# Start addresses of matmul operands in SBUF, brought to one offset modulo 2 KB

## The chip, the cores and the metric

One Trainium2 chip, one of its cores. The metric is the device time of one execution of the whole program in microseconds, as the median of repeated runs: 3694.65 us before (3 runs, 3694.28 to 3696.64). The profile comes from one more execution.

## What is computed

Two blocks follow each other on 256 tokens of width 2048, in float32. Cut to the large products:

```python
# first block
xn = rmsnorm(x, g)
p_rw, q, c_kv, iq, ik, iw, gates = split(xn @ w_in)            # 2048 x 9320
y_a = rwkv7_time_mix(p_rw, ...) @ w_branch_rwkv                # 1024 x 2048
y_b = dsa_attention(q, c_kv, iq, ik, iw, ...) @ w_branch_dsa   # 1024 x 2048
h = x + (g_a * y_a + g_b * y_b) @ w_out                        # 2048 x 2048
s = (h @ w_query) against sub_keys; top 16 of 16384 experts per token and head
h = h + peer(h, expert_u, expert_v)                            # two 16384 x 2048 tables
# second block
z, xbc, dt = split(x @ a_w_in)                                 # 2048 x 10304
x = layernorm(ALPHA * x + mamba2(z, xbc, dt) @ a_w_out)        # 4096 x 2048
k, v = shared_kv(x @ kv_w); q, gate = split(x @ b_w_in)        # 2048 x 4096
out = layernorm(ALPHA * x + (attend(q, k, v) * silu(gate)) @ b_w_out)  # 2048 x 2048
```

The expert layer is computed over all 16384 experts: `act = gelu(h @ u.T)`, times a dense table of gates, times `v`.

## The kernel before, in words

Each large product is made of float32 numbers that are split into a rounded part (`hi`, or the first half of a row of `x2`) and the rest (`lo`, or the second half). TensorE takes two operands from SBUF: a stationary one of 128x128, which is loaded ahead of the matmul, and a moving one, which streams 512 or 256 columns. A partition's row of 512 float32 numbers is 2048 bytes.

There are three shapes of this work.

- `gemm` (L171, matmuls on L205 and L207). A weight chunk is loaded into `raw` (`wload`, L144), ScalarE writes its rounded part into `hi` (L140), VectorE the rest into `lo` (L142). `hi` and `lo` are stationary, 128 columns at a time; the moving operand is a row of an activation tile of [128, k, 512]: 256 tokens rounded and 256 tokens of rest. A matmul with `hi` streams 512 columns, the one with `lo` the first 256. So matmuls of 512 and 256 columns alternate. The activation tile is `x2` in most products, and `o2b`, `br_a`, `m2`, `xq` and `y2m` in five of them. The first product over the expert table (`Peer.up`, L1171, matmuls on L1203 and L1204) has the same pattern with `x2`, on transposed weights (tile `tr`, written by L1184, split on L140 and L142).
- `Peer.down` (L1231, matmuls on L1250 to L1252). Here `g2`, the product of activation and gate (in buffers of the tag `tr`, L1266), is stationary, and `hi` and `lo` of the expert rows move, 512 columns in every matmul: `hi`, `lo`, and `hi` again for the second half of `g2`.
- `gemm_rows` (L214, matmuls on L228 to L230), the last product. `o2` is stationary, `hi` and `lo` move, 512 columns in three products of the output's columns and 256 in two.

`second` and `ffn` (from L1887 and L2000) run under a scheduler that fixes each engine's order when the program is built; the rest runs in the order of the code. Tiles are placed in SBUF by pools in the order in which the pools and their tiles are made: `const`, `wp` (with `raw`, `hi`, `lo`), `tp`, then `act` with `x2`. Their start addresses follow from the sizes of what was placed ahead of them.

```python
hi = self.wp.tile([128, 2, 512], F32R, tag="hi", bufs=HL_BUFS, name="hi")          # L158
nc.tensor.matmul(ps[f], lhsT=hi[:, k, f * 128:(f + 1) * 128], rhs=x2[:, q, :], ...)  # L205
nc.tensor.matmul(ps[f][:, 0:T], lhsT=lo[:, k, f * 128:(f + 1) * 128], rhs=x2[:, q, 0:T], ...)  # L207
nc.tensor.matmul(p, lhsT=x, rhs=hi, start=first, stop=False)                        # L1250
nc.tensor.matmul(p, lhsT=x, rhs=lo, start=False, stop=False)                        # L1251
nc.tensor.matmul(p, lhsT=g2[:, T + tt * 128:T + tt * 128 + 128], rhs=hi, ...)       # L1252
```

Of the kernel before, what the change touches and what calls it, by code (L numbers as in the profile page):

```python
# [9 lines left out]
F32 = mybir.dt.float32  # L10
F32R = mybir.dt.float32r
# [9 lines left out]
T = 256  # L21
D = 2048
KT = D // 128
# [87 lines left out]
class K:  # L111
    def __init__(self, tc, es, a):
        self.scheduled = False
        self.tc, self.nc, self.es, self.a = tc, tc.nc, es, a
        self.const = es.enter_context(tc.tile_pool(name="const", bufs=1))
        self.wp = es.enter_context(tc.tile_pool(name="wp", bufs=1))
        self.gp = es.enter_context(tc.tile_pool(name="gp", bufs=6, space=PSUM))
        self.mp = es.enter_context(tc.tile_pool(name="mp", bufs=2, space=PSUM))
        self.tp = es.enter_context(tc.tile_pool(name="tp", bufs=1))
        tc.nc.scalar.preload_act_table_set("natural_log_exp_and_others")  # L120
        self.c = self.load_consts(self.const, "const_f", _GEN)
        self.ident = self.c["ident"]

    def load_consts(self, pool, name, d):
        t = pool.tile([128, sum(x.shape[1] for x in d.values())], F32, name=name)
        self.nc.scalar.dma_start(t, self.a[name])
        out, o = {}, 0
        for n, x in d.items():
            out[n] = t[:, o:o + x.shape[1]]
            o += x.shape[1]  # L130
        return out
# [862 lines left out]
class Peer:  # L994
    def __init__(self, k, hn2, pool, h_d):
        self.k, self.hn2, self.pool, self.tr, self.h_d = k, hn2, pool, pool, h_d
        self.anchor = {}
        self.pI = [pool.tile([128, T], F32, name=f"pI{i}") for i in range(3)]
        self.ni1, self.nw = (pool.tile([128, T], F32, name=f"pN{i}") for i in range(2))
        self.iota = pool.tile([128, 128], F32, name="iota")  # L1000
        k.nc.gpsimd.iota(self.iota, pattern=[[1, 128]], base=0, channel_multiplier=0,
                         allow_small_or_imprecise_dtypes=True)
# [295 lines left out]
def alternate(a, b):  # L1298

    live = [a, b]  # L1300
    while live:
        for x in list(live):
            if next(x, "end") == "end":
                live.remove(x)
            else:
                yield


def peer(k, x2, xq, norm, hh, h_d, g_d, act_d, acts, es, finish):

    tc = k.tc
    pp = es.enter_context(tc.tile_pool(name="peer", bufs=1))
    pe = Peer(k, x2, pp, h_d)
    scores = hh[:, 0].rearrange("p k t -> p (k t)").rearrange("p (a j n) -> p a j n", a=2, j=16)
    with tc.tile_pool(name="query", bufs=1) as qp:
        pe.query(qp, xq, *norm(qp), scores)
    scr = acts.tile([128, 4, 2048], F32, tag="act0", name="scr")
    two = scr.rearrange("p (a b) f -> p a (b f)", a=2)  # L1320
    with tc.tile_pool(name="up", bufs=1) as up:
        pe.pool = up
        main = pe.up(act_d)
        route = [pe.route(up, tt) for tt in range(2)]
        gates = [pe.gates(tt, two, g_d, act) for tt, act in enumerate(GATE_ACT)]
        side = pe.anchored(itertools.chain(route[0], alternate(route[1], gates[0]), gates[1]))
        R, G, due = pe.ROUTE_STEPS, 34, 0.0
        rates = [R / UP_PLAN[0]] * UP_PLAN[0] + [(R + G) / UP_PLAN[1]] * UP_PLAN[1] + [G / UP_PLAN[2]] * UP_PLAN[2]
        for r in rates:
            next(main)  # L1330
            due += r
            while due >= 1:
                due -= 1
                next(side, None)
        for _ in side:
            pass
        for _ in main:
            pass
    with tc.tile_pool(name="down", bufs=1) as dp:
        pe.pool = dp  # L1340
        for _ in pe.down(scr, act_d, g_d, hh[:, 0], finish(hh[:, 0], dp)):
            pass
    return hh.rearrange("p a k t -> p (a k) t")
# [543 lines left out]
def second(k, hx, x2, ssq, g, es, out):  # L1887


    tc, nc, a = k.tc, k.nc, k.a  # L1890
    cp = es.enter_context(tc.tile_pool(name="cpar", bufs=1))
    x = hx[:, 0:KT]
    rs = cp.tile([128, T], F32, name="rs_x")
    ssq.rstd(D, 1e-6, rs)
    par = k.params("par2", par2_plan(a), cp)

    def scale(j):

        nc.vector.scalar_tensor_tensor(x[:, j], x[:, j], g[:, j:j + 1], rs, op0=ALU.mult, op1=ALU.mult)

    with tc.tile_pool(name="yp", bufs=1) as yp, tc.tile_pool(name="zph", bufs=1) as zp:
        m = Mamba(k, par, rs, hx, yp, zp)
        W = a["a_w_in_2"][0]
        with tc.tile_pool(name="mb", bufs=1) as mb:
            m.setup(mb)
            k.gemm(x2, KT, W, [(8192 + 512 * i, 4) for i in range(2)], m.evict_xbc)
            k.gemm(x2, KT, W, [(10176, 1)], m.evict_dt)
            k.gemm(x2, KT, W, [(9216 + 512 * i, 4) for i in range(2)], m.evict_xbc)
            side = None
            for i in range(8):  # L1910
                k.gemm(x2, KT, W, [(4096 + 512 * i, 4)], m.evict_xbc, side=side)
                side = (m.group(i), 2, 2)
                with k.tc.issue_after(m.mark.ins):
                    scale(2 * i)
                    scale(2 * i + 1)
            k.gemm(x2, KT, W, [(0, 4)], m.evict_z, side=side)
        with tc.tile_pool(name="y2p", bufs=1) as y2p:
            m.y2 = y2 = y2p.tile([128, 32, 2 * T], F32R, name="y2m")
            for i in range(1, 8):
                k.gemm(x2, KT, W, [(512 * i, 4)], m.evict_z, side=(m.norm(i - 1), 3, 1))  # L1920
            ln = Ln(k, x, zp, cp, par["ln_g"][:, 0:16], par["ln_b"][:, 0:16])
            k.gemm(y2, 32, a["a_w_out_2"][0], [(512 * i, 4) for i in range(3)] + LAST, ln.evict,
                   side=(m.norm(7), 3, 1))
            with tc.manual_schedule():
                head = k.head(a["kv_w_2"], 0, 512)
                ln.stats()
    yield
    with tc.tile_pool(name="o2p", bufs=1) as op:
        o2 = op.tile([128, 16, 2 * T], F32R, name="o2")
        with tc.tile_pool(name="sw", bufs=1) as sp:  # L1930
            s = Swa(k, par, sp, hx[:, 16:32])
            W = a["b_w_in_2"][0]
            k.gemm(x2, KT, a["kv_w_2"], [(0, 4)], s.evict_kv, side=(itertools.chain(ln.finish(x2), s.tables()), 0, 1),
                   head=head, fixed=True)
            k.gemm(x2, KT, W, [(512 * i, 4) for i in range(4)], s.evict_q)
            s.attend()
            rows = hx[:, 16:32].rearrange("p (a k) t -> p a (k t)", a=2)
            k.gemm(x2, KT, W, [(2048 + 512 * i, 4) for i in range(4)], s.evict_gate(o2, lambda j: ln.residual(rows, j)))
        with tc.tile_pool(name="fin", bufs=1) as fp:
            lr = LnRows(k, fp, [a[n][1:2, :] for n in ("ln_g_2", "ln_b_2")], out)  # L1940
            for c, n in ((0, 512), (512, 512), (1024, 512), (1536, 256), (1792, 256)):
                k.gemm_rows(o2, KT, a["b_w_out_2"][0], [(c, n)], lr.evict(rows))
            lr.finish(rows)
# [89 lines left out]
def body(tc, a, out):  # L2033
    with ExitStack() as es:
        k = K(tc, es, a)
        pool = lambda n, side=None: es.enter_context(tc.tile_pool(name=n, bufs=1, side=side))
        act = pool("act")
        dram = es.enter_context(tc.tile_pool(name="dram", bufs=1, space=DRAM))
        x2 = act.tile([128, KT, 2 * T], F32R, name="x2")
        keep = ExitStack(), ExitStack(), ExitStack()  # L2040
        par, *state = first(k, x2, dram, keep, pool)
        with tc.block(schedule_with_timeline_sim=True):
            k.scheduled = True
            hx, ssq = ffn(k, x2, par, *state, keep, dram)
            fin = second(k, hx, x2, ssq, par["norm_final_g"], es, out)
            next(fin)
            k.scheduled = False
        next(fin, None)
# [31 lines left out]
```

## Time and profile before

| | us |
|---|---|
| median of 3 runs | 3694.65 |
| the profiled execution's own time | 3696.7 |
| its span, first to last instruction | 3694.9 |
| PE busy | 3570.3 (97%) |
| DVE busy | 2617.8 (71%) |
| ACT busy | 2030.2 (55%) |
| POOL busy | 1323.9 (36%) |
| mean granted TensorE clock | 0.992 of full speed |

The profiled execution lies 2.05 us above the median, and 1.8 us of its time lie outside the span. PE is TensorE's matmul side, PEld its weight loads, DVE VectorE, ACT ScalarE, POOL GpSimd. A busy PE is not a PE at its peak, since matmuls overlap and their ends are modelled: how fast TensorE goes is read from the starts of successive matmuls, or from how many of them stand in a stretch.

### The profile page before, as it was taken

To read this page: it belongs to the slowest core of one execution; us is meant where nothing else is said; L and a number is where in the kernel's file an instruction comes from. 1 tells how busy PE (TensorE), PEld (TensorE's weight loads), DVE (VectorE), ACT (ScalarE), POOL (GpSimd) and SP (SyncE) were. 2 spreads that over 40 slices of the span, in tenths; PEclk is the share of its full clock that TensorE was granted. 3 is DMA by queue.
4 is the path that set the end of the run, shared out by engine and by line. 5 is a ranking of instruction groups with operands and counts; after the bars stand their busy time and mean duration, and the time that the engine had idled before them with its cause. 6 is when DMAs were issued, how large, how long until landed. Compare 5 with 4: busy or idle time off the path is not lost.

```text
span 3694.9 us, 55970 instructions
## 1 busy us (share of the span) xinstructions
PE 3570.3 (97%) x19751; PEld 2991.5 (81%) x19751; DVE 2617.8 (71%) x4165; ACT 2030.2 (55%) x3861; POOL 1323.9 (36%) x1339
## 2 busy tenths in 40 slices
PE   9999999999999999998899999999999999989998
PEld 7678888878888888887788888888788887878777
DVE  5766777667588888788644444446899879667766
ACT  5555556545454677766544444445555667444674
POOL 1333223211288777755511111111234544142001
PEclk9999999999999999999999999999999999999999
DMA  7444434477698888878977777765554445645434
GB/s 221 138 160 129 131 122 132 140 230 244 172 204 207 201 213 221 219 180 208 253 246 237 229 235 231 221 200 187 164 172 145 141 139 171 192 145 184 144 120 149
DMA packets 377277, 681.21 MB, mean 184 GB/s; under 512 B 44493, under 2 KB 128373, under 8 KB 375845
## 3 DMA queue, kind: packets, MB, share of 16 engines
q1 hardware_dynamic: 343104, 625.05, 58.0%
q10 hardware_dynamic: 33893, 52.58, 4.2%
q8 instruction: 156, 2.56, 0.3%
q14 instruction: 124, 1.02, 0.1%
HBM read 627.57 MB, written 47.22 MB: 183 GB/s over the span
## 4 chain that ended last, share of the span: by engine, by line
PE 45%; DVE 3%; ACT 1%; DMA 1%; issue 1%; POOL 0%; SPq 0%; ACTq 0%; DVEq 0%; POOLq 0%
PE g L205 13%; PE g L207 7%; PE gv L1250 5%; PE gv L1251 5%; PE gv L1252 5%; PE dv L1252 2%; PE dv L1250 2%; PE dv L1251 2%; DVE lo L142 1%; PE g L229 1%; PE g L228 1%; PE g L230 1%; ACT hi L140 1%; PE psl L1840 1%; DMA raw<-in_peer_u_dram 1%
## 5 line engine op out<-in xcount | busy, mean ns | idle before, releaser
L142 DVE TENSOR_TENSOR lo<-raw,hi 128x1024 fp32r<-128x1024 f32 (+3 forms) x856 | 1039.3, 1218 | 622.6 <-ACT hi L140 618.7
L140 ACT CAST hi<-raw 128x1024 fp32r<-128x1024 f32 (+3 forms) x858 | 867.3, 1013 | 908.3 <-PE gv L1252 395.8
L205 PE MATMUL g<-x,hi 128*128 128x512 f32 x3040 | 1091.2, 401 | 13.0 <-DVE x L1662 9.0
L207 PE MATMUL g<-x,lo 128*128 128x256 f32 x3040 | 844.0, 288 | 16.7 <-DVE lo L142 16.5
L1203 PE MATMUL gu<-x,hi 128*128 128x512 f32 x2048 | 733.0, 398 | 1.7 <-ACT hi L140 1.7
L142 POOL TENSOR_TENSOR lo<-tr,hi 128x512 fp32r<-128x512 f32 x429 | 589.2, 1401 | 250.8 <-ACT hi L140 175.2
L205 PEld LDWEIGHTS g<-x,hi 128*128 128x128 f32 x3040 | 568.3, 189 | 133.0 <-issue 19.8
L207 PEld LDWEIGHTS g<-x,lo 128*128 128x128 f32 x3040 | 575.0, 189 | 53.0 <-DVE lo L142 26.9
L1204 PE MATMUL gu<-x,lo 128*128 128x256 f32 x2048 | 580.2, 284 | 30.4 <-POOL lo L142 27.3
L1203 PEld LDWEIGHTS gu<-x,hi 128*128 128x128 f32 x2048 | 386.4, 189 | 88.6 <-ACT hi L140 2.4
L1204 PEld LDWEIGHTS gu<-x,lo 128*128 128x128 f32 x2048 | 386.7, 189 | 48.5 <-POOL lo L142 44.7
L1184 DVE STREAM_TRANSPOSE tr<-raw 128x1024 f32<-128x1024 f32 x256 | 309.0, 1231 | 90.6 <-POOL lo L142 43.8
L140 ACT CAST hi<-tr 128x512 fp32r<-128x512 f32 x512 | 290.0, 616 | 76.2 <-PE gu L1203 54.5
L142 POOL TENSOR_TENSOR g<-scr,g 128x512 fp32r<-128x512 f32 x64 | 114.9, 1797 | 572.0 <-ACT g L140 572.0
L1252 PE MATMUL gv<-hi,g 128*128 128x512 f32 x756 | 299.7, 396 | 0.0
L1251 PE MATMUL gv<-lo,g 128*128 128x512 f32 x756 | 299.7, 396 | 0.0
L1250 PE MATMUL gv<-hi,g 128*128 128x512 f32 x756 | 238.4, 396 | 0.0
L1212 ACT ACTIVATE act<-act 128x256 f32<-128x256 f32 x128 | 53.4, 417 | 222.6 <-DVE act L241 222.3
L205 PE MATMUL g<-y2m,hi 128*128 128x512 f32 x512 | 175.2, 397 | 0.3 <-ACT hi L140 0.3
L1251 PEld LDWEIGHTS gv<-lo,g 128*128 128x128 f32 x756 | 142.4, 188 | 34.7
L1252 PEld LDWEIGHTS gv<-hi,g 128*128 128x128 f32 x756 | 142.4, 188 | 34.7
L1250 PEld LDWEIGHTS gv<-hi,g 128*128 128x128 f32 x756 | 142.4, 188 | 34.7
(604 smaller groups left out, 5856.4 us busy)
## 6 DMA issues: line engine op xcount, KB each, us to landing
raw<-in_peer_u_dram SPq DMA_DIRECT2D x512, 256.0 KB
raw<-in_peer_v_dram SPq DMA_DIRECT2D x256, 512.0 KB
raw<-in_a_w_in_dram SPq DMA_DIRECT2D x160, 512.0 KB
raw<-in_w_in_dram SPq DMA_DIRECT2D x136, 512.0 KB
raw<-in_b_w_in_dram SPq DMA_DIRECT2D x64, 512.0 KB
raw<-in_a_w_out_dram SPq DMA_DIRECT2D x48, 512.0 KB
raw<-in_w_out_dram SPq DMA_DIRECT2D x32, 512.0 KB
raw<-in_w_peer_query_dram SPq DMA_DIRECT2D x32, 512.0 KB
```

The costliest lines, as they stand in the source:

```text
L140: ins = nc.scalar.copy(hi, x) if heng == "act" else nc.vector.tensor_copy(hi, x)
L142: return ins, eng.tensor_tensor(lo, x, hi.bitcast(F32), op=ALU.subtract)
L205: nc.tensor.matmul(ps[f], lhsT=hi[:, k, f * 128:(f + 1) * 128], rhs=x2[:, q, :], start=(q == 0), stop=False)
L207: nc.tensor.matmul(ps[f][:, 0:T], lhsT=lo[:, k, f * 128:(f + 1) * 128], rhs=x2[:, q, 0:T], start=False, stop=(q == nk - 1))
L228: nc.tensor.matmul(ps[tt], lhsT=x, rhs=w, start=(q == 0), stop=False)
L1184: st["t"] = nc.vector.transpose(tr.rearrange("p b (u j) -> p u b j", u=2), raw[:, 2 * u:2 * u + 2].rearrange("p u (b j) -> p u b j", j=32))
L1203: nc.tensor.matmul(ps, lhsT=hi[:, j], rhs=self.hn2[:, q, :], start=(q == 0), stop=False)
L1204: st["m"] = nc.tensor.matmul(ps[:, 0:T], lhsT=lo[:, j], rhs=self.hn2[:, q, 0:T], start=False, stop=(q == KT - 1))
L1212: nc.scalar.activation(o, o, AF.Gelu)
L1250: nc.tensor.matmul(p, lhsT=x, rhs=hi, start=first, stop=False)
L1251: nc.tensor.matmul(p, lhsT=x, rhs=lo, start=False, stop=False)
L1252: nc.tensor.matmul(p, lhsT=g2[:, T + tt * 128:T + tt * 128 + 128], rhs=hi, start=False, stop=last)
```

## The change

The tile `x2` and the pool `wp` are made first, ahead of `const`. Two unused pads are added, of 352 bytes per partition ahead of the expert layer's tiles and of 448 ahead of `o2`. Two tiles of 1 KB (`ni1`, `nw`) move from the pool that lives through the whole expert layer to the one that lives through its first half.

```diff
 class K:
     def __init__(self, tc, es, a):
+        self.x2 = es.enter_context(tc.tile_pool(name="act", bufs=1)).tile([128, KT, 2 * T], F32R, name="x2")
+        self.wp = es.enter_context(tc.tile_pool(name="wp", bufs=1))
         self.const = es.enter_context(tc.tile_pool(name="const", bufs=1))
-        self.wp = es.enter_context(tc.tile_pool(name="wp", bufs=1))
...
+    def pad(self, pool, n):
+        pool.tile([128, n // 4], F32, name="pad")
...
 class Peer: (__init__)
+        k.pad(pool, 352)
         self.pI = [pool.tile([128, T], F32, name=f"pI{i}") for i in range(3)]
-        self.ni1, self.nw = (pool.tile([128, T], F32, name=f"pN{i}") for i in range(2))
...
 def peer(...):
     with tc.tile_pool(name="up", bufs=1) as up:
         pe.pool = up
+        pe.ni1, pe.nw = (up.tile([128, T], F32, name=f"pN{i}") for i in range(2))
...
 def second(...):
     with tc.tile_pool(name="o2p", bufs=1) as op:
+        k.pad(op, 448)
         o2 = op.tile([128, 16, 2 * T], F32R, name="o2")
...
 def body(tc, a, out):
-        act = pool("act")
-        x2 = act.tile([128, KT, 2 * T], F32R, name="x2")
+        x2 = k.x2
```

In the built programs each engine has the same instructions in the same order, with the same waits. What differs is where tiles stand. The start of a tile's row in its partition, in bytes modulo 2048, is

| tile | part in the matmul | before | after |
|---|---|---|---|
| `x2` | moving in `gemm` and `up` | 288 | 128 |
| `hi`, `lo` | stationary in `gemm` and `up`, moving in `down` and `gemm_rows` | 1728 | 128 |
| `g2` | stationary in `down` | 1824 | 128 |
| `o2` of the last product | stationary in `gemm_rows` | 1728 | 128 |
| `xq`, `o2b`, `br_a` | moving in `gemm` | 288 | 288 |
| `m2` | moving in `gemm` | 2016 | 2016 |
| `y2m` | moving in `gemm` | 704 | 704 |

A stationary piece of 128 columns is 512 bytes, so its own start is the tile's plus a multiple of 512.

## Rows read from the trace of the kernel before

**Rows 1.** The page: span, busy time by engine, granted clock by slice, chain that ended last.
```profile
span 3694.9 us, 55970 instructions
...
PE 3570.3 (97%) x19751; PEld 2991.5 (81%) x19751; DVE 2617.8 (71%) x4165; ACT 2030.2 (55%) x3861; POOL 1323.9 (36%) x1339
...
PEclk9999999999999999999999999999999999999999
...
PE 45%; DVE 3%; ACT 1%; DMA 1%; issue 1%; POOL 0%; SPq 0%; ACTq 0%; DVEq 0%; POOLq 0%
```

**Rows 2.** Groups by line and shape, PE: busy us, mean ns; idle before.
```profile
L205 PE MATMUL g<-x,hi 128*128 128x512 f32 x3040 | 1091.2, 401 | 13.0 <-DVE x L1662 9.0 <-ACT hi L140 3.8 <-DVE x L979 0.2
...
L1203 PE MATMUL gu<-x,hi 128*128 128x512 f32 x2048 | 733.0, 398 | 1.7 <-ACT hi L140 1.7
...
L1251 PE MATMUL gv<-lo,g 128*128 128x512 f32 x756 | 299.7, 396 | 0.0
...
L1251 PE MATMUL dv<-lo,g 128*128 128x512 f32 x252 | 99.9, 396 | 0.0
```

**Rows 3.** Stretches of steady work on PE: us, PE busy (instructions), granted clock, DMA.
```profile
core 0: us, PE busy (x), PEclk, DMA share, GB/s
41.84:99.94 58.10, 58.10 (x334) 1.00 0.78 204
836.17:841.37 5.20, 5.20 (x32) 1.00 1.06 372
1840.00:2550.00 710.00, 710.00 (x3032) 1.00 0.70 226
3174.80:3204.83 30.03, 30.03 (x173) 1.00 0.62 199
3219.93:3250.08 30.15, 30.15 (x176) 1.00 0.53 169
3640.39:3657.39 17.00, 17.00 (x77) 1.00 0.56 185
3658.00:3680.00 22.00, 22.00 (x186) 1.00 0.44 142
```

**Rows 4.** Timeline of PE, a piece of `gemm` with `x2`: start us, us.
```profile
50.24 0.39 PE L205 MATMUL g<-x,hi 128*128 128x512 f32 x1
50.47 0.28 PE L207 MATMUL g<-x,lo 128*128 128x256 f32 x1
50.59 0.39 PE L205 MATMUL g<-x,hi 128*128 128x512 f32 x1
```

**Rows 5.** Groups by line in 1840 to 2550 us, the second expert product.
```profile
L142 DVE TENSOR_TENSOR lo<-raw,hi 128x1024 fp32r<-128x1024 f32 x250 | 305.2, 1224 | 311.1 <-ACT hi L140 310.4
...
L140 ACT CAST hi<-raw 128x1024 fp32r<-128x1024 f32 x251 | 264.1, 1052 | 404.3 <-PE gv L1252 395.8 <-DVE scr L1265 3.5 <-DMA raw<-in_peer_v_dram 2.5
```

**Rows 6.** Waits of PE over the span: us in total, times, longest.
```profile
PE gu L1204 <- POOL lo L142: 27.3, 39, 2.0
PE g L207 <- DVE lo L142: 21.5, 25, 2.2
```

**Rows 7.** Busy time of each engine in 1000 to 1840 us, the first expert product.
```profile
core 0: us, PE busy (x) PEld busy (x) DVE busy (x) ACT busy (x) POOL busy (x), PEclk, DMA share, GB/s
1000.00:1840.00 840.00, 804.73 (x4655) 694.90 (x4654) 699.25 (x1129) 534.03 (x1235) 597.73 (x439) 0.99 0.86 210
```

**Rows 8.** Groups by tile on PE: `y2m` in `gemm`.
```profile
L205 PE MATMUL g<-y2m,hi x512: 387/395/582, 3109.7 to 3296.9; 128*128 128x512 f32 x171
```

## Prediction

> **What bounds the kernel now.** I read the page first, for what the end waits for. PE is busy for 3570.3 of 3694.9 us, no other engine for more than 71%, and in the chain that ended last PE has by far the largest engine share, 45% against 3% for DVE and 1% each for ACT and the DMAs; the granted clock is at nine tenths or more in every slice, which is the upper of TensorE's two levels, 2.4 GHz [rows 1]. So time is gained or lost where successive matmuls start closer together or farther apart, or where PE stands idle.
>
> Next come the groups by line, but a matmul's own duration there doesn't answer the question: it is some 400 ns for 512 columns [rows 2], while the timeline shows the next but one starting after 0.35 us [rows 4]. Matmuls overlap. I therefore take stretches without a stall, and divide their length by the matmuls in them. A window counts what was still running when it began, and sometimes one that starts on its end, so one to three are taken off each count:
>
> - `gemm` with `x2`: 58.10 us hold 166 pairs of a 512 and a 256 column matmul, 350.0 ns per pair.
> - `gemm` with `m2`: 5.20 us, 15 pairs, 346.7 ns.
> - `gemm` with `y2m`: 30.03 us, 85 pairs, 353.3 ns; later 30.15 us, 87 pairs, 346.6 ns.
> - `Peer.down`: 710.00 us, 3031 matmuls of 512 columns, 234.3 ns each.
> - `gemm_rows`: 17.00 us, 75 matmuls of 512 columns, 226.7 ns each; 22.00 us with 256 columns, 120 ns.
>
> The granted clock is 1.00 in all of these [rows 3]. At 2.4 GHz 512 columns take 213.3 ns and a pair's 768 take 320 ns. So the excess over the columns is 21 ns a matmul in `down`, 13.4 in `gemm_rows`, and 27 to 33 a pair elsewhere. This excess is all that an address could act on.
>
> Now the same five against the addresses in the table of starts. What I choose to compare is the stationary operand's start less the moving one's, modulo 512, since a stationary piece is 512 bytes. It is 1728 - 288 = 1440, so 416, for `x2`; 224 for `m2`; 1024, so 0, for `y2m`; 1824 - 1728 = 96 for `down`; 0 for `gemm_rows`. Two things stand out. `gemm_rows` and `down` run the same shape, 512 columns with three matmuls in a round, and the one with equal starts is 7.6 ns faster. And `y2m`, with equal starts, is no better off on average than `x2`: on one set of addresses it runs at 346.6 for a while and at 353.3 for another, mean 350.0. So the start alone does not fix a pair's pitch.
>
> **The change, part by part.** No instruction, order or wait changes; the pads and the moved `ni1` and `nw` issue nothing and cost nothing. Only operand reads can become faster or slower.
>
> *Down.* The difference goes from 96 to 0, as `gemm_rows` has it. The main groups are 3 x 756 + 3 x 252 = 3024 matmuls, from the counts at the line of `lo` [rows 2]. Bounds: 0, if the 7.6 ns have another cause, and 3024 x (234.3 - 213.3) = 63 us if the whole excess went. I take the nearest row, `gemm_rows`: 3024 x 7.6 ns = **-23.0 us**. All of it is on the path: in this stretch PE is busy for 710.00 of 710.00 us [rows 3], and ACT, which makes `hi`, waits 395.8 us for PE to give the buffer back [rows 5]; VectorE's `lo` waits for ACT in turn. A PE that is 3% faster eats into these waits. The loads must then come at 226 x 234.3/226.7 = 234 GB/s, and 372 GB/s were reached at `m2` [rows 3]. So nothing else becomes late.
>
> Here a rule speaks against the gain. The Trainium skill ("SBUF — State Buffer", "Who interferes with whom") gives PE one read port for the moving operand and one for loading the stationary one, calls them independent, and says that PE never waits on anyone. By that rule no start address would matter, and the sum would be 0. The traces agree with it only in part: a pitch of 234.3 beside 226.7 ns for like matmuls at one clock [rows 3] needs some cause, though two stages differ in more than addresses.
>
> *`x2`, in `gemm` and `up`.* 3040 + 2048 = 5088 pairs [rows 2], difference 416 to 0. The nearest row with the same alternation of 512 and 256 columns and a difference of 0 is `y2m`, whose mean is 350.0 ns: no change, **0**. Its two levels are the bounds: 5088 x 3.3 ns = 17 us either way. In `up` PE is idle for 35 of 840 us, largely waiting for POOL's `lo`, 27.3 us in 39 waits; in `gemm` 21.5 us of waits for DVE's `lo` [rows 6, 7]. A faster pair would give a part of its gain back there. POOL is busy for only 597.73 of the 840 us [rows 7], so I leave the bound whole.
>
> *The other moving operands.* `hi` and `lo` move, while `xq`, `o2b`, `br_a`, `m2` and `y2m` stay: the difference becomes 352 for the first three, 160 for `m2` and 448 for `y2m`. Pairs: 512 for `y2m` [rows 8], and 752 for the rest by the shapes of their products (256 for `xq` and `m2` each, 128 for `o2b`, 112 for `br_a`). I take 0, bounded by 1264 x 3.3 ns = 4 us either way.
>
> *`gemm_rows`.* Difference 0 before and after: 0.
>
> *Splits.* ACT, DVE and POOL read and write `raw`, `hi` and `lo`, which move together; 1224 and 1052 ns for a chunk's `lo` and `hi` in `down` [rows 5] are taken as unchanged.
>
> Sum: -23.0 us. The profiled execution took 3696.7 us, 2.05 above the median; it becomes 3673.7, and the median 3694.65 - 23.0 = **3671.6 us**.
>
> **Rivals.**
>
> 1. *The pairs with `x2` settle on the lower level too.* `y2m` shows that 346.6 can be had with equal starts, and `m2` has it as well [rows 3]. Against it, `y2m` fell to 353.3 on the same addresses. Then 17 us more: 3671.6 - 17 = 3654.6. Chance 0.22.
> 2. *Down gains, but `x2` settles on the upper level*: 353.3 ns, +17 us, net -6: 3688.6, within what a measurement tells from no change. Chance 0.07.
> 3. *No effect: the change doesn't do what it is for.* `down` and `gemm_rows` differ in more than their addresses: 3000 matmuls without a stall against runs of a hundred or two, 226 against 185 GB/s of loads [rows 3]. For it: the mean of `y2m` equals that of `x2` at quite another difference. 3694.65, chance 0.10.
> 4. *Slower: equal starts make the two reads fall on the same place at the same time.* The mechanism is in the loop on L205 and L207: while `x2`'s row streams, the next piece of `hi` or `lo` is loaded. The level of 353.3 ns, the highest pitch of a pair, was seen only at difference 0 [rows 3]. If `x2` goes there and `down` stays at 234.3, the time is 3694.65 + 17 = 3711.6. It decides once the loss per pair of `x2` times 5088 exceeds the gain per matmul of `down` times 3024, that is, from 4.5 ns a pair on if `down` gains its 7.6, and from any loss on if `down` gains nothing. Chance 0.06.
> 5. *All excess over the columns goes.* 63 us in `down` and 30 ns x (5088 + 1264) = 191 us in the pairs: about 3441. No stretch shows so low a pitch, not even `gemm_rows` with equal starts. Chance 0.02.
>
> The Trainium skill ("TensorE: Matmul & The Clock Gate", "Wait — 56ns, not 53.3ns?") gives 215.7 ns from start to start for 512 columns of a warm array, which would be nearly all of that; no stretch here shows it.
>
> **How the numbers follow.** The forecast keeps 0.53. A measurement of this kernel tells about 0.2%, 7.4 us, from no change. Faster: the forecast, rivals 1 and 5, 0.77. Same: rivals 2 and 3, 0.17. Slower: 0.06. The range should take in the forecast and rival 1 in full, and below rival 1 the 4 us of the other operands and the 2 us by which the runs before differ: 3654.6 - 6, about 3648. Upward it reaches to rival 2 at 3688.6, say 3689. Left out are rivals 3 to 5, 0.18.
>
> **What would show it.** In the second expert product 710 us should hold some 3130 matmuls instead of 3031, at 226.7 ns. A stretch of `gemm` with `x2` should show 350 ns a pair on average, possibly as pieces at 347 and at 353; if it shows one of these throughout, rival 1, 2 or 4 holds. `m2`, `xq`, `o2b`, `br_a` and `y2m` should lie between 346 and 354. The means of `hi` and `lo` on ACT, DVE and POOL should stand within 1%. I am wrong if `down` stays at 234 ns, if the gain in `down` returns as PE idle time behind `hi` or a load, or if a pair leaves the band of 346 to 354.

## The result, and the profile after

The changed kernel takes **3667.49 us** (median of 4 runs, 3664.07 to 3668.66) against 3694.47 of the kernel before in the same comparison: 27.0 us less, a ratio of 0.9925 with a 95% interval of 0.9908 to 0.9942. Forecast were 3671.6 us, 23.0 less, in a range from 3648 to 3689.

The profile's page of the changed kernel answers to [rows 1]:

```profile
span 3665.9 us, 55970 instructions
...
PE 3542.2 (97%) x19751; PEld 2990.1 (82%) x19751; DVE 2615.5 (71%) x4165; ACT 2030.5 (55%) x3861; POOL 1330.2 (36%) x1339
...
PEclk9999999999999999999999999999999999999999
...
PE 45%; DVE 4%; ACT 1%; DMA 1%; issue 1%; POOL 0%; SPq 0%; DVEq 0%; ACTq 0%; POOLq 0%
```

The same instructions, the same granted clock, and PE still the engine of the end. The span is 29.0 us shorter and PE's busy time 28.1 us; no other engine's busy time moved by more than 7. So the time came from the spacing of the matmuls, and the question is from which.

Stretches without a stall, as in [rows 3] (columns: the stretch in us, PE busy with its instructions, granted clock, DMA share, GB/s). They are, in order, `gemm` with `x2`, with `m2` and with `xq`, the second expert product, `y2m` twice, and 512 columns of the last product:

```profile
41.00:99.30 58.30, 58.30 (x333) 1.00 0.77 203
864.50:877.50 13.00, 13.00 (x76) 1.00 0.95 307
963.00:977.00 14.00, 14.00 (x83) 1.00 0.56 175
1835.00:2515.00 680.00, 680.00 (x3001) 1.00 0.72 233
3145.00:3175.00 30.00, 30.00 (x173) 1.00 0.62 200
3193.00:3223.00 30.00, 30.00 (x174) 1.00 0.52 160
3610.00:3627.00 17.00, 17.00 (x77) 1.00 0.58 186
```

Less the one to three that were under way or start on the end, the second expert product holds 3000 matmuls in 680 us, **226.7 ns** each, where it took 234.3 [rows 3]. That is to the tenth what the last product had, and still has (75 in 17 us). The pairs went both ways. In this stretch `x2` is at 165 pairs in 58.30 us, 353.3 ns, where it was at 350.0 [rows 3]; `y2m` shows two levels once more, 85 pairs and 86 in 30 us.

Whole stages, from the first matmul of one to the first of the next (or to the last of its own), show where the 29.0 us of the two spans lie. For the second expert product first the kernel before, then the changed one (columns now with every engine):

```profile
1836.70:2555.90 719.20, 719.20 (x3074) 578.40 (x3072) 348.79 (x316) 302.88 (x321) 108.57 (x60) 1.00 0.71 227
```

```profile
1830.90:2527.00 696.10, 696.10 (x3073) 576.42 (x3072) 347.59 (x316) 303.38 (x321) 108.74 (x60) 1.00 0.72 234
996.80:1830.80 834.00, 797.16 (x4642) 689.64 (x4642) 697.07 (x1127) 533.52 (x1233) 600.83 (x439) 0.99 0.83 211
```

| stretch | before, us | after, us | difference |
|---|---|---|---|
| up to `m2` | 805.6 | 803.5 | -2.1 |
| `m2` and `xq` | 193.8 | 193.3 | -0.5 |
| first expert product | 837.2 | 834.0 | -3.2 |
| second expert product | 719.2 | 696.1 | -23.1 |
| all behind it | 1139.0 | 1138.9 | -0.1 |

The second expert product gave 23.1 us. The 5.9 us of the rest are spread over stages that differ by 2 to 3 us between two executions of one kernel: the changed kernel, profiled a second time (after_again, below), took 806.1 us up to `m2` and 1142.2 behind the second expert product. One execution can't tell them from nothing; ten runs of x2_only, below, can.

That nothing else became late there is told by two groups of the stage, answering to [rows 5]:

```profile
L146 ACT CAST hi<-raw 128x1024 fp32r<-128x1024 f32 x248 | 261.6, 1055 | 378.8 <-PE gv L1258 365.8 <-DMA raw<-in_peer_v_dram 11.3 <-DVE lo L148 1.7
...
L148 DVE TENSOR_TENSOR lo<-raw,hi 128x1024 fp32r<-128x1024 f32 x249 | 302.8, 1225 | 287.0 <-ACT hi L146 286.9
```

ScalarE and VectorE need the same time for a chunk (1055 and 1225 ns); they merely wait less, 365.8 instead of 395.8 us for PE in stretches of 680 and 710 us. The wait for a load grew from 2.5 to 11.3 us and did not reach PE, which has no gap in the stretch (680.00 of 680.00 us).

### The profile page after: what moved, and what is told of

It reads as the page before. It is cut to its first block, busy times and chain, and to the rows that moved or that the text cites. A ratio compares the mean times of both kernels' runs of the same rounds, so it can differ in the third digit from the quotient of the medians.

```text
span 3665.9 us, 55970 instructions
## 1 busy us (share of the span) xinstructions
PE 3542.2 (97%) x19751; PEld 2990.1 (82%) x19751; DVE 2615.5 (71%) x4165; ACT 2030.5 (55%) x3861; POOL 1330.2 (36%) x1339
## 4 chain that ended last, share of the span: by engine, by line
PE 45%; DVE 4%; ACT 1%; DMA 1%; issue 1%; POOL 0%; SPq 0%; DVEq 0%; ACTq 0%; POOLq 0%
PE g L211 13%; PE g L213 7%; PE gv L1258 5%; PE gv L1256 5%; PE gv L1257 5%; PE dv L1256 2%; PE dv L1258 2%; PE dv L1257 2%; DVE lo L148 1%; PE g L235 1%; PE g L234 1%; PE g L236 1%; ACT hi L146 1%; PE psl L1847 1%; DMA raw<-in_peer_u_dram 1%
## 5 line engine op out<-in xcount | busy, mean ns | idle before, releaser
L146 ACT CAST hi<-raw 128x1024 fp32r<-128x1024 f32 (+3 forms) x858 | 868.0, 1014 | 890.0 <-PE gv L1258 365.8
L148 POOL TENSOR_TENSOR lo<-tr,hi 128x512 fp32r<-128x512 f32 x429 | 591.0, 1405 | 245.0 <-ACT hi L146 161.3
L1258 PE MATMUL gv<-hi,g 128*128 128x512 f32 x756 | 294.1, 389 | 0.0
L1256 PE MATMUL gv<-hi,g 128*128 128x512 f32 x756 | 232.7, 389 | 0.0
```

Source lines behind the costliest of these rows:

```text
L146: ins = nc.scalar.copy(hi, x) if heng == "act" else nc.vector.tensor_copy(hi, x)
L148: return ins, eng.tensor_tensor(lo, x, hi.bitcast(F32), op=ALU.subtract)
```

## The experiments

A kernel is named by three differences: the stationary operand's start less the moving one's, modulo 512, in the products with `x2`, in the second expert product, and in the last product. Before: 416, 96, 0. Changed: 0, 0, 0. The theory under test was that this difference sets the pitch (A). Its rivals: starts must be equal modulo 2048 (B); the absolute place of a tile counts (C); the level of a pair is drawn anew after each stall, whatever the addresses (D).

### Each half of the change alone

**down_only** (416, 0, 0; `g2` at 192, `hi` at 1728 modulo 2048) is the kernel before with

```diff
+        pool.tile([128, 416 // 4], F32, name="pad")
         self.pI = [pool.tile([128, T], F32, name=f"pI{i}") for i in range(3)]
-        self.ni1, self.nw = (pool.tile([128, T], F32, name=f"pN{i}") for i in range(2))
...
         pe.pool = up
+        pe.ni1, pe.nw = (up.tile([128, T], F32, name=f"pN{i}") for i in range(2))
```

> Down alone: the kernel before with a pad of 416 bytes ahead of the expert layer's tiles (and ni1 and nw moved, for room). g2 then starts at 192 and hi and lo at 1728 modulo 2048: equal modulo 512, 512 apart modulo 2048; x2 and all else stand as before. Theory A, the difference of the two starts modulo 512 sets the pitch: 226.7 ns in the second expert product, the stretch 23 us shorter, 3694.5 - 23 = 3671.5. Rival B, the starts must be equal modulo 2048: 234.3 ns, 3694.5. Rival C, what helped was g2 standing at 128 modulo 2048, whatever hi and lo stand at: 234.3 ns or another value that is not 226.7.

Measured: 3670.31 us against 3695.44, ratio 0.9933 (0.9918 to 0.9948), 25.1 us less. The stretch in the second expert product:

```profile
1840.00:2520.00 680.00, 680.00 (x3002) 1.00 0.73 233
```

3000 matmuls in 680 us, 226.7 ns. A holds for 512 columns. B and C are out there: the two starts are 512 apart modulo 2048, and neither is where the change puts it.

**x2_only** (0, 96, 0) is the changed kernel with

```diff
-        k.pad(pool, 352)
+        k.pad(pool, 448)
```

> The change without its part for down: the first pad is 448 instead of 352 bytes, so that g2 starts 96 bytes beyond hi modulo 512, as before the change; x2 stays aligned. Theory A: 234.3 ns in the second expert product, 3667.5 + 23 = 3690.5, and the 4 us that remain against the kernel before are spread over the stages with x2, xq, o2b and br_a. Rival B (absolute place of x2, hi and lo at 128 modulo 2048 is what counts): below 234 ns there, 3667 to 3672. Pairs with x2 as in the changed kernel: pieces at 347, 350 and 353 ns, mean 349 to 350.

Measured: 3691.49 us (10 runs, 3685.54 to 3696.38) against 3695.44, ratio 0.9990 (0.9980 to 0.9999). The same stretch:

```profile
1840.00:2520.00 680.00, 680.00 (x2904) 1.00 0.71 227
```

2903 in 680 us, 234.2 ns: 96 bytes bring the old pitch back. The rest of the change, that is `x2` together with `xq`, `o2b`, `br_a` and `m2`, is worth 4 us, between 0.4 and 7.4. The halves, 25.1 and 4.0, add up to the whole, 27.0, within their intervals.

### Other differences

**x2_224** (224, 0, 0) adds a pad behind `x2`; **sweep_a** to **sweep_d** do the same with other sizes, and change the two pads of the change too:

```diff
-        self.x2 = es.enter_context(tc.tile_pool(name="act", bufs=1)).tile([128, KT, 2 * T], F32R, name="x2")
+        act = es.enter_context(tc.tile_pool(name="act", bufs=1))
+        self.x2 = act.tile([128, KT, 2 * T], F32R, name="x2")
+        self.pad(act, 224, "pad1")
...
-    def pad(self, pool, n):
+    def pad(self, pool, n, name="pad"):
-        pool.tile([128, n // 4], F32, name="pad")
+        pool.tile([128, n // 4], F32, name=name)
```

> The changed kernel with a pad of 224 bytes between x2 and the pool of raw, hi and lo: the stationary start less that of x2 is 224 modulo 512, as m2 had it before the change, where it kept 346.7 ns. Down and the last product stay aligned with each other. Theory A: pairs with x2 at 346.7 ns in every stretch without a stall, from a mean of 350.0 in gemm and 349.1 in up, so 3040 x 3.3 + 2048 x 2.4 = 15 us less at most, 3653 to 3658. Rival B (equal starts are best for pairs too): 350 ns or more, 3667 or above. Rival D (the level of a pair is drawn anew after each stall, whatever the addresses): the mixture of the changed kernel again, 3664 to 3669.

Measured: 3665.23 us (3663.10 to 3665.55) against 3695.44, ratio 0.9920 (0.9906 to 0.9933), where the changed kernel had 0.9925: not told apart. The time is the one that rival D had, not the 3653 to 3658 of A. Yet the pitch did what A says, in `gemm` and in the first expert product:

```profile
40.00:92.00 52.00, 52.00 (x302) 1.00 0.83 222
...
1022.50:1066.00 43.50, 43.50 (x252) 1.00 0.87 203
```

150 pairs in 52 us and some 125 in 43.5 are 346.7 and 348 ns, the first expert product's with the short gap between two experts' blocks. Most of the expected gain didn't reach the end; where it stayed is the question of "Why the first expert product did not get shorter".

**sweep_a** (64, 256, 96):

> One look at three other differences, each read in its own stage: x2 at 64, down at 256, the last product at 96 (the changed kernel with pads of 64 bytes behind x2, 608 ahead of the expert layer's tiles, 544 ahead of o2). Theory A: the last product, so far at 226.7 ns, takes down's old pitch of 234.3 ns in stretches without a stall, 288 x 7.6 = 2.2 us more; down at 256, half a piece away, is the farthest from equal: 234 ns or above, some 23 us more or above; x2 between 346 and 354 ns. Rival C (the absolute place decides): the last product stays at 226.7.

**sweep_b** (96, 32, 128):

> Differences x2 96, down 32, last product 128 (the changed kernel with pads of 96 bytes behind x2, 384 ahead of the expert layer's tiles, 576 ahead of o2). So far, for 512 columns: 0 and 256 gave 226.7 ns, 96 gave 234.3. Theory A64, the remainder of the difference by 64 decides (0 good, 32 bad): down 234.3 ns, last product 226.7. Theory A256, only a difference near 0 modulo 256 is good: down at 32 between 226.7 and 234.3, last product at 128 as bad as 234 or worse. For pairs, 224 and 352 kept 346.7 ns and 160 and 416 kept 350.0, which are 96 and 32 modulo 128: by theory P128 x2 at 96 keeps 346.7; if only 224 and 352 themselves are good, x2 lies at 350 or above.

**sweep_c** (32, 64, 160):

> Differences x2 32, down 64, last product 160, m2 192. Theory A64: down 226.7 ns, last product 234.3. Theory A256: down above 230. Theory P128: x2 at 32 keeps 350.0 ns (349 and 351 in the timeline), as 160 and 416 did; m2 at 192, which is 64 modulo 128, shows the mixture of levels that x2 at 64 and y2m at 448 did, 350 to 353.

**sweep_d** (256, 128, 32):

> Differences x2 256, down 128, last product 32, m2 416. Theory A64: down 226.7 ns, last product 234.3. Theory A256: down at 128 the worst of all, 234 or above. Theory P128: x2 at 256 like at 0, a mixture of pieces at 347, 350 and 353, mean 349 to 350; m2 at 416 keeps 350.0, as x2 did before the change.

One execution each gave 3675.80, 3685.98, 3703.31 and 3682.77 us; they are read by their stages. The second expert product in steady stretches, of sweep_a, with a stretch of its last product behind it:

```profile
1845.00:2525.00 680.00, 680.00 (x3002) 1.00 0.73 233
...
3618.00:3636.00 18.00, 18.00 (x79) 1.00 0.55 176
```

of sweep_b (first `gemm` with `x2`):

```profile
42.00:94.00 52.00, 52.00 (x301) 1.00 0.78 221
1840.00:2540.00 700.00, 700.00 (x3002) 1.00 0.71 226
```

of sweep_c:

```profile
41.00:99.30 58.30, 58.30 (x332) 1.00 0.77 208
1850.00:2550.00 700.00, 700.00 (x3002) 1.00 0.71 227
```

and of sweep_d:

```profile
41.00:99.30 58.30, 58.30 (x331) 1.00 0.79 209
1835.00:2535.00 700.00, 700.00 (x3015) 1.00 0.71 227
```

Counted in the same way:

| difference | 512 columns, second expert product | pairs, `x2` near the start of the program |
|---|---|---|
| 0 | 226.7 ns (changed) | 353.3, elsewhere 346.7 (changed) |
| 32 | 233.3 (sweep_b) | 353, elsewhere 346.8 (sweep_c) |
| 64 | 233.3 (sweep_c) | 353.3 (sweep_a: 165 pairs in 58.30 us) |
| 96 | 234.3 (before, x2_only) | 346.7 (sweep_b) |
| 128 | 232.3 (sweep_d) | |
| 224 | | 346.7 (x2_224) |
| 256 | 226.7 (sweep_a) | 353.3, elsewhere 346.7 (sweep_d) |
| 416 | | 350.0 (before) |

The second level at 0, 32 and 256 stands in later stretches with `x2`, of the changed kernel, sweep_c and sweep_d:

```profile
725.00:751.00 26.00, 26.00 (x152) 1.00 0.68 223
```

```profile
1025.00:1068.00 43.00, 43.00 (x249) 1.00 0.87 202
```

```profile
721.00:747.00 26.00, 26.00 (x152) 1.00 0.69 224
```

For 512 columns the period is **256 bytes** as far as these differences go, not the 512 that I had taken from the size of a stationary piece: 256 is as good as 0, and 128 is bad. Between 128 and 256 nothing was tried in this product. A64, that the remainder by 64 decides, fell: 32 was bad as it said, but so were 64 and 128. A256, that only a difference near 0 modulo 256 is good, held, save that 128 is not the worst. The last product agrees: misaligned by 96 in sweep_a it went to 77 in 18 us, the 234 ns of the second expert product; rival C had it at 226.7. At 160, in sweep_c, it shows the same count,

```profile
3645.50:3663.50 18.00, 18.00 (x79) 1.00 0.55 176
```

and so it does at 128 and at 32, in sweep_b and sweep_d (x79 in 18 us each). Absolute places make no difference: with 0 modulo 256, `hi` stood at 128, 192, 352 (x2_224, x3002 in 680 us) and 1728 modulo 2048 and the pitch was 226.7 each time.

For pairs equal starts are not the best: 96 and 224 are, and 64 is worse than what was there before. P128, that 32 behaves like 160 and 416, was wrong: 32 gave no steady 350.0. All that was seen of pairs agrees with a period of 256: `m2` at 160 runs like `x2` at 416, and `xq` at 352 like `x2` at 96. As expected, `m2` kept 350 ns at 416 in sweep_d and showed more than one level at 192 in sweep_c. Short stretches are better read from the starts than counted, since one matmul more or less in 14 us is 4 ns of a pair; here are `xq` before the change (24 pairs from the first start to the last, 350.0 ns), `xq` after it (17 pairs, 346.5) and `m2` after it (15 pairs, 350.0):

```profile
989.75 0.39 PE L205 MATMUL g<-xq,hi 128*128 128x512 f32 x1
...
998.15 0.39 PE L205 MATMUL g<-xq,hi 128*128 128x512 f32 x1
```

```profile
989.62 0.39 PE L211 MATMUL g<-xq,hi 128*128 128x512 f32 x1
...
995.51 0.39 PE L211 MATMUL g<-xq,hi 128*128 128x512 f32 x1
```

```profile
857.96 0.39 PE L211 MATMUL g<-m,hi 128*128 128x512 f32 x1
...
863.21 0.39 PE L211 MATMUL g<-m,hi 128*128 128x512 f32 x1
```

At most differences it was one product and one execution, so the period of the pairs rests on less than that of 512 columns.

### Every product at its best difference

**all_best** is x2_224 with

```diff
+            k.pad(y2p, 96)
             m.y2 = y2 = y2p.tile([128, 32, 2 * T], F32R, name="y2m")
...
         m2 = mp.tile([128, KT, 2 * T], F32R, name="m2")
+        k.pad(mp, 96)
```

and **after_again** is the changed kernel once more.

> x2_224 with m2 moved by 96 bytes (difference 480, so 224 modulo 256) and y2m by 96 (352, so 96 modulo 256): every moving tile of gemm and up stands at a difference of 96 or 224 modulo 256, the two that kept 346.7 ns, while down and the last product keep 0. Theory (the difference modulo 256 decides, 96 and 224 are the best for pairs): m2 back from 351 to 346.7-347.4 ns and y2m from 350 to about 347, so 256 x 3.7 + 512 x 3 = 2.5 us less than x2_224, and 7 us less than the changed kernel in gemm with x2; together 9 us below the changed kernel of the same call, about 3659 if that is at 3668. Rival (levels are drawn anew after each stall whatever the address): within 3 us of the changed kernel.

> The changed kernel again, on the same chip as the others of this call, as their yardstick: 3664 to 3670.

Measured: 3664.26 us, ratio 0.9918 (0.9905 to 0.9932), and 3667.77 us, ratio 0.9919 (0.9905 to 0.9932). The medians stand 3.5 us apart, the ratios 0.0001: no version that beats the changed kernel measurably, and no 9 us. The pitches are there: `y2m` now at 150 pairs in 52 us throughout, `m2` at some 15 in 5.2.

```profile
3145.00:3197.00 52.00, 52.00 (x302) 1.00 0.60 189
840.90:846.10 5.20, 5.20 (x31) 1.00 0.70 232
994.40:1830.70 836.30, 794.98 (x4641) 0.99 0.86 211
```

The last row is the first expert product: 836.3 us, though its pairs keep the lower level and those of the changed kernel change between two, and the changed kernel's stage took 834.0.

### Why the first expert product did not get shorter

Over all kernels above this stage took 832 to 841 us (847.5 in sweep_c, which stays unexplained), and the kernels with the lowest pitch did not have the shortest stage: 837.2 at 416, 834.0 at 0, 835.6 and 836.3 at 224, 838.0 at 96, 840.7 at 64. The other stages, without the two expert products, did get a little shorter: 2129.5 us in x2_224, against 2135.7 in the changed kernel and 2140.8 in after_again, where at most 3040 x 3.3 ns = 10 us were expected. These are single executions; nolo_0, below, took 2129.7 us there at difference 0.

The waits in the changed kernel's stage name a chain (engine and work that waited, for whom, us in total, times, longest):

```profile
ACT act L1218 <- DVE act L247: 217.9, 95, 5.3
POOL lo L148 <- ACT hi L146: 161.3, 110, 5.7
ACT hi L146 <- PE gu L1209: 55.2, 64, 3.1
DVE tr L1190 <- POOL lo L148: 51.5, 25, 4.9
PEld gu L1210 <- POOL lo L148: 46.6, 53, 2.4
```

POOL is busy for 600.83 of the 834.00 us and waits another 161.3 for `hi` from ScalarE, which itself stands behind VectorE's `act` in its own queue. So at a busy share of 72% POOL has little to spare, and PE's weight loads wait for it. Two kernels take POOL out by leaving out the part of this product that `lo` carries: **nolo_0** from the changed kernel and **nolo_224** from x2_224, both with

```diff
-            hi, lo = (k.wp.tile([128, 8, 128], F32R, tag=n, bufs=HL_BUFS, name=n) for n in ("hi", "lo"))
+            hi = lo = k.wp.tile([128, 8, 128], F32R, tag="hi", bufs=HL_BUFS, name="hi")
...
-                st["h"], st["l"] = k.split(tr[:, 8 * c:8 * c + 8], hi[:, :, d], lo[:, :, d], leng="dve" if dve else "pool")
+                st["h"] = st["l"] = k.nc.scalar.copy(hi[:, :, d], tr[:, 8 * c:8 * c + 8])
```

> The changed kernel without lo in the first expert product: the split writes only hi, and the second matmul takes hi in place of lo (this leaves out the part of the product that lo carries). POOL's 429 and DVE's 83 subtractions there are gone. To be compared with nolo_224. Theory: POOL and the chain behind it set the pace of this stage in most places, so that a lower pitch of PE's pairs comes back as waiting; without lo the stage is PE's alone, some 2048 x 349 to 351 ns = 715 to 719 us and the stalls that remain, instead of 834.

> x2_224 with the same cut, lo left out of the first expert product (this leaves out the part of the product that lo carries). Theory (POOL's chain hid the gain): the stage is shorter than in nolo_0 by the difference of the pitches, 2048 x 2.4 to 4 ns = 5 to 8 us, where x2_224 was 1.6 us longer than the changed kernel. Rival (the lower pitch is not worth anything in this stage, whoever else is in the way, for instance since the loads of the table set the pace): the same length within 2 us.

Measured: 3610.81 and 3608.83 us; the stage, nolo_0 first, then nolo_224:

```profile
993.60:1776.50 782.90, 777.34 (x4642) 688.31 (x4642) 522.96 (x1044) 534.63 (x1233) 9.26 (x10) 0.99 0.90 224
```

```profile
996.50:1777.60 781.10, 775.09 (x4642) 691.84 (x4642) 520.79 (x1043) 534.48 (x1233) 9.26 (x10) 1.00 0.92 224
```

Without `lo` the stage is 834.0 - 782.9 = 51 us shorter in nolo_0 and 835.6 - 781.1 = 54.5 us in nolo_224, at the same number of matmuls. The second of these is the cleaner comparison, since pairs at 224 keep 346.7 ns with and without `lo`: POOL's and VectorE's subtractions, or what waits behind them, had cost PE that much. So it is shown that PE's pitch was not the stage's only limit; which of POOL, ScalarE's queue and VectorE comes first was not separated. My 715 to 719 us were too low, since they left out the stage's other 4642 - 4096 = 546 matmuls and the stalls that stay.

The test that I had meant failed: the two lengths differ by 1.8 us, not 5 to 8. That is within the 2 us of the rival, but it does not show the rival either, since the pitches hardly differ any more. Here is a steady stretch of nolo_0, and behind it one of the changed kernel with the same starts of `x2` and `hi`:

```profile
1020.00:1220.00 200.00, 200.00 (x1155) 1.00 0.90 217
```

```profile
1030.00:1100.00 70.00, 70.00 (x397) 1.00 0.88 212
```

577 pairs in 200 us are 346.6 ns; 198 in 70 us are 353.5. At difference 0 the pair has two levels, as `y2m` had before, and without the stalls for `lo` the lower one was met and kept for 200 us. Leaving out `lo` is not what makes the level, though: each of the two kernels has both. In the changed kernel 15 pairs stand in 5.20 us, 346.7 ns, just ahead of the slow stretch, with one stall for `lo` between them:

```profile
1020.00:1025.20 5.20, 5.20 (x32) 1.00 0.99 223
```

And in nolo_0 six pairs take 2.08 us ahead of a small matmul of another kind, 346.7 ns, and six take 2.12 behind it, 353.3:

```profile
1223.84 0.39 PE L1209 MATMUL gu<-x,hi 128*128 128x512 f32 x1
...
1225.92 0.39 PE L1209 MATMUL gu<-x,hi 128*128 128x512 f32 x1
...
1226.27 0.27 PE L1121 MATMUL psr<-const_f,res 128*128 128x128 f32 x1
...
1226.73 0.40 PE L1209 MATMUL gu<-x,hi 128*128 128x512 f32 x1
...
1228.85 0.40 PE L1209 MATMUL gu<-x,hi 128*128 128x512 f32 x1
```

So D is half right: the difference of the starts decides which levels there are, and at 0 the level can change where the stream of pairs is interrupted. What in an interruption picks the level was not separated. At 96 and 224 I saw only the lower one in steady stretches with `x2`.

## Why the prediction was right

The mechanism that the forecast rests on is the one that the runs showed: 96 bytes between the two starts in the second expert product.

*Down.* Forecast -23.0 us from `gemm_rows`' pitch; measured -23.1 in the profiled stage and -25.1 (ratio interval 0.9918 to 0.9948) with this half alone. The nearest row was the right one to take, and its pitch was met to a tenth of a nanosecond. "Nothing else becomes late" held: loads came at 233 GB/s, 234 foreseen.

The Trainium skill ("SBUF — State Buffer", "Who interferes with whom") says that the moving operand and the weight load have independent read ports and that PE never waits on anyone. If independent means that the start of the one does not matter to the other, the runs disagree for this kernel: 96 bytes between the two starts make 512 columns 7.6 ns slower (down_only and x2_only). How the two reads meet inside the memory no run here shows.

*`x2`.* Forecast 0, within 17 us either way; measured 4 us less with this half alone, 0.4 to 7.4, the other operands included. The whole change gave 4.0 us more than forecast, about this much. The pairs did mix the two levels of `y2m`, as its mean said. Rivals 1 and 2, that one level is kept throughout, did not come true at difference 0; rival 1's level is to be had at 96 and 224.

*A step that was wrong, within a right sum:* "POOL is busy for only 597.73 of the 840 us, so I leave the bound whole." In the first expert product a lower pitch brought no shorter stage (835.6 and 836.3 us in x2_224 and all_best against 834.0). The 4.5 ns condition of the rival on the slower side never came near, as `down` gained its whole 7.6.

*Another:* the modulus. I compared starts modulo 512. The answer did not hang on it, since 0 is 0 in either, but the measured period is 256: a change from 96 to 256 would have been forecast as no gain, as the expectation of sweep_a has it, and would have gained as much. Nothing of 2 KB was needed.

*The other operands.* Forecast 0; `xq` went from 350 to 346.5 ns and `m2` from 347 to 350, in the band of 346 to 354, too small to be seen in the total.

## What to carry to other kernels

Where PE is the bound and two streams of the same shape differ in pitch, compare the start addresses of stationary and moving operands before anything else: here a pad of some hundred bytes took 0.7% off the program, with no instruction moved. Measure the best difference per shape: equal starts modulo 256 were right for 512 columns after 512, but 512 and 256 in turn ran closer at 96 and 224, though the whole program did not gain by that measurably. And read a stage's limit from who waits for whom; the busy share of an engine that stands in a chain says too little.

## What the runs showed of the hardware

At one set of addresses a stream can have several pitches: with equal starts pairs ran at 346.6 ns for 200 us in nolo_0, at 353.5 for 70 us in the changed kernel, and each of the two kernels has both levels, on either side of an interruption. A mean over such pieces, 350.0 for `y2m`, is not a pitch that the hardware has there. Whether an address is good for pairs therefore takes several stretches to tell, while for 512 columns one stretch was enough: in the second expert product the pitch was steady over the 680 to 710 us shown of each kernel.
